# Putting the routing stretch of a two-layer trunk kernel into written order

## The chip, the cores and the metric

One core of one Trainium2 chip runs the kernel. The metric is the device time of one execution in microseconds (us); lower is better. A core has five engines with queues of their own: PE (TensorE, matrix multiplication), DVE (VectorE), ACT (ScalarE), POOL (GpSimd) and SP (SyncE, which here only issues transfers). Each works through its own queue in order and waits on semaphores for the others.

## The reference, cut to what matters

Two layers (`DEPTH = 2`) over 512 tokens of width 1024. Each adds a token mixer and then a PEER block, which alone is touched here:

```python
q = (xt @ wq).reshape(t, 8, 2, 128)
scores = einsum('thcd,hcnd->thcn', q, sub_keys)       # two times 128 keys for each of 8 heads
sv, si = top_k(scores, 16)
cand = sv[:, :, 0, :, None] + sv[:, :, 1, None, :]    # 16 x 16 sums
best_s, best_p = top_k(cand, 16)
idx  = take(si0 * 128 + si1, best_p)                  # 16 of 16384 experts for each head
gate = softmax(best_s)
act  = einsum('td,thkd->thk', x, u_tab[idx])
y    = einsum('thk,thkd->td', gelu(act) * gate, v_tab[idx])
```

Inputs and outputs are fp32; 128 (token, expert) pairs for each token.

## The kernel before

The tokens are four tiles of 128 (`t` = 0 to 3). For tiles 0 to 2 (384 tokens) the kernel doesn't gather: it multiplies them with the whole table of experts, 128 experts at a time, and a map of gates (zero where a token didn't choose an expert) selects. For tile 3 it gathers the rows of the chosen experts.

- A **U block** `e` (0 to 127): SP loads 512 KB of `peer_ut` (`uload`, L672, three buffers `u_raw`); ACT copies it to a rounded part `u_hi` and DVE subtracts to get `u_lo` (`uprep`, L677, two buffers each); PE runs 24 matmuls of 128x384 (`uact`, L702: in turn `xh`*`u_hi`, `xl`*`u_hi`, `xh`*`u_lo`); ACT applies gelu and, for `e` < 60, its queue issues the store of the result to DRAM (`ge`, L712).
- **Selection** (`stage2(t)`, L771) for the tiles in the order 3, 0, 1, 2, nearly all on DVE: candidate sums (L777 to 785), for each of 8 heads five instructions for the best 16 (L792 to 796), softmax and the arithmetic that takes a position apart (L799 to 822, with one exp on ACT), comparison and summing trees over 4096 columns (L825 to 840), normalisation (L841 to 844). For tiles 0 to 2 PE transposes the result (L852, L853) and DVE casts it to bf16 (L855 to 860: `idxT`, `gateT`).
- **Gate maps** (`onehots(t)`, L863): 24 batches of 16 tokens. DVE builds two comparison maps `oeq` and three maps `oag` of 128x2048 bf16 for a batch (L875, L879). PE multiplies them four tokens at a time, 12 matmuls of 128x128 (L885; here called a quad, four to a batch); ACT moves each quad to a staging tile `st` (L888). After two batches, a **chunk**, ACT's queue stores 2 MB to `gd` (L890).
- **Gathers** for tile 3 (`gather_u`, L731): POOL gathers one row per token (512 KB) into one of four buffers, DVE multiplies it with the token and sums it into `act` (L736). Buffers 0 and 1 of the four are the scores' own tile `sbuf`, free once selection has read it.
- **V phase** (from L969): the remaining U blocks and 128 V blocks (`vmm`, L957), written by hand under `tc.manual_schedule()`.

Up to L910 the order on each engine comes from the tile framework's scheduler, which takes instructions that it thinks ready by priority and an estimate of durations. The program only sets a pace: each `yield` of `stage2` and `onehots` gives a credit (`W_S`, `W_O / 2`), and `paced` (L893) writes a U block into the program each time the credit reaches one. By L910 that makes 69 blocks (33 beside selection, 36 beside the maps); four more (69 to 72) stand at L970, before the first V block. The V phase below is executed in its written order.

Of the kernel before, what the change touches and what calls it, by code (L numbers as in the profile page):

```python
# [7 lines left out]
F32 = mybir.dt.float32  # L8
F32R = mybir.dt.float32r
BF16 = mybir.dt.bfloat16  # L10
# [7 lines left out]
P = 128  # L18
# [29 lines left out]
W_S = 1.25  # L48
W_O = 0.75
G_R = 1  # L50
G_B = 1
# [16 lines left out]
def trunk_kernel(ctx: ExitStack, tc: tile.TileContext, x, norm1_g, w_in, sb_qn_g, sb_kn_g, ml_conv_w,  # L68
# [598 lines left out]
    def layer(l):  # L667
        with ExitStack() as pctx:
# [8 lines left out]
            def uprep(e):  # L677
                if e < NK:
                    uh = pools["up"].tile([P, ND, P], F32R, name="u_hi")
                    ul = pools["up"].tile([P, ND, P], F32R, name="u_lo")  # L680
                    src = uraw.pop(e)
                    nc.scalar.activation(uh, src, AF.Copy)  # L682
                    nc.vector.tensor_sub(ul, src, uh.bitcast(F32))  # L683
                    uT[e] = (uh, ul)
# [79 lines left out]
            with ExitStack() as bctx:  # L764
# [4 lines left out]
                pace = {"e": 0, "credit": 0.0}  # L769

                def stage2(t):  # L771
                    sv, si = svs[t], sis[t]
# [13 lines left out]
                    yield W_S  # L786
                    bs = tk.tile(HK, F32, name="bs", bufs=2)
                    bp = tk.tile(HK, U32, name="bp", bufs=2)
                    for h in range(PH):
                        c1 = cand[:, h]  # L790
                        c2 = tk.tile([P, 64], F32, name="c2", bufs=2)
                        nc.vector.max(bs[:, h, :8], c1)  # L792
                        nc.vector.max_index(bp[:, h, :8], bs[:, h, :8], c1)
                        nc.vector.match_replace(c2, bs[:, h, :8], c1, LOW)  # L794
                        nc.vector.max(bs[:, h, 8:], c2)
                        nc.vector.max_index(bp[:, h, 8:], bs[:, h, 8:], c2)
                        if h % 4 == 3:
                            yield W_S
# [24 lines left out]
                    yield W_S  # L823
# [6 lines left out]
                    yield W_S  # L830
# [3 lines left out]
                    yield W_S  # L834
# [10 lines left out]
                    if t == NT - 1:  # L845
                        nc.vector.tensor_scalar(ii[:, 0], ii[:, 0], float(NK), float(l * NE), op0=ALU.mult,
                                                op1=ALU.add)
                        nc.vector.tensor_add(idx, ii[:, 0], ii[:, 1])
                        return
                    pt = ps.tile([P, S], F32, name="tr", bufs=1)  # L850
                    for c in range(2):
                        nc.tensor.transpose(pt[:, c * P:(c + 1) * P], ii[:, c], ident)  # L852
                    nc.tensor.transpose(pt[:, 2 * P:3 * P], gt.rearrange("p h k -> p (h k)"), ident)  # L853
                    ts_ = slice(t * P, (t + 1) * P)
                    nc.vector.tensor_copy(idxT[:, :, ts_], pt[:, :2 * P].rearrange("p (c t) -> p c t", c=2))  # L855
                    gr = tk.tile([P, P], F32, name="gr", bufs=2)
                    nc.vector.tensor_copy(gateT[:, 0, ts_], pt[:, 2 * P:3 * P])
                    nc.vector.tensor_sub(gr, pt[:, 2 * P:3 * P], gateT[:, 0, ts_])
                    nc.vector.tensor_copy(gateT[:, 1, ts_], gr)
                    nc.vector.tensor_sub(gateT[:, 2, ts_], gr, gateT[:, 1, ts_])  # L860
                    yield W_S

                def onehots(t):  # L863
                    QS = [P, OT // 2, NK, 2]
                    for c in range(P // TC):
                        st = stg.tile([P, NK, TC], F32, name="st")
                        for b in range(TC // OT):
                            t0 = t * P + c * TC + b * OT

                            def pairs(row):  # L870
                                return row[:, t0:t0 + OT].rearrange("p (q b) -> p q b", b=2)[:, :, None, :].to_broadcast(QS)

                            eq = oh.tile([P, 2] + QS[1:], BF16, name="oeq")
                            for i in range(2):
                                nc.vector.tensor_tensor(eq[:, i], iota_t[:, None].to_broadcast(QS), pairs(idxT[:, i]),  # L875
                                                        op=ALU.is_equal)
                            ag = [oh.tile(QS, BF16, name="oag", bufs=4) for _ in range(3)]
                            for i in range(3):
                                nc.vector.tensor_mul(ag[i], eq[:, 0], pairs(gateT[:, i]))  # L879
                            for b4 in range(OT // 4):  # L880
                                pg = ps.tile([P, 4, NK], F32, name="oh", bufs=3)
                                for k in range(4):
                                    q, r = divmod(b4 * 4 + k, 2)
                                    for i in range(3):
                                        nc.tensor.matmul(pg[:, k, :], eq[:, 1, q, :, r], ag[i][:, q, :, r],  # L885
                                                         start=(i == 0), stop=(i == 2))
                                o = b * OT + b4 * 4
                                nc.scalar.activation(st[:, :, o:o + 4].rearrange("p i t -> p t i"), pg, AF.Copy)  # L888
                                yield W_O / 2
                        nc.scalar.dma_start(gd[t * (P // TC) + c, :, :NK * TC],  # L890
                                            st.rearrange("p i t -> p (i t)"))

                def paced(steps):  # L893
                    for n, w in enumerate(steps):
                        pace["credit"] += w
                        while pace["credit"] >= 1 and pace["e"] < UB:
                            uphase(pace["e"], ps)
                            pace["e"] += 1
                            pace["credit"] -= 1
                        yield n  # L900

                for _ in paced(w for t in (NT - 1, *range(NT - 1)) for w in stage2(t)):
                    pass
                tkctx.close()
                with ExitStack() as octx:
                    oh = octx.enter_context(tc.tile_pool(name="oh", bufs=2))
                    stg = octx.enter_context(tc.tile_pool(name="stg", bufs=2))
                    for n in paced(w for t in range(NT - 1) for w in onehots(t)):
                        gather(G_B * (n % 2))
                u_tail = pace["e"]  # L910

            with ExitStack() as cctx:
# [55 lines left out]
                with tc.manual_schedule():  # L968
                    uload(u_tail + 2)  # L969
# [66 lines left out]
```

## Time and profile before

| | |
|---|---|
| median of 3 runs | 3234.32 us (3233.31 to 3236.99) |
| the profiled execution's own time | 3247.25 us |
| its span | 3245.5 us |
| PE busy | 3142.2 us (97%) |
| DVE busy | 2480.4 us (76%) |
| ACT busy | 1381.0 us (43%) |
| POOL busy | 679.9 us (21%) |
| granted PE clock, mean | 0.98 of full speed |

The shares are means over very different stages. The change touches one stage in each layer, some 420 us long; it is the rows of that stage, which stand further down, that have to be read. In every row of a timeline the first number is the start from the span's beginning, the second the duration, both in us; in square brackets stands how long the engine was idle before and what released it. Successive instructions of one engine overlap by a little: the distance between two starts is what an instruction costs its queue.

### The profile page before, as it was taken

To read this page: it belongs to the slowest core of one execution; us is meant where nothing else is said; L and a number is where in the kernel's file an instruction comes from. 1 tells how busy PE (TensorE), PEld (TensorE's weight loads), DVE (VectorE), ACT (ScalarE), POOL (GpSimd) and SP (SyncE) were. 2 spreads that over 40 slices of the span, in tenths; PEclk is the share of its full clock that TensorE was granted. 3 is DMA by queue.
4 is the path that set the end of the run, shared out by engine and by line. 5 is a ranking of instruction groups with operands and counts; after the bars stand their busy time and mean duration, and the time that the engine had idled before them with its cause. 6 is when DMAs were issued, how large, how long until landed. Compare 5 with 4: busy or idle time off the path is not lost.

```text
span 3245.5 us, 46361 instructions
## 1 busy us (share of the span) xinstructions
PE 3142.2 (97%) x17496; PEld 2784.1 (86%) x17496; DVE 2480.4 (76%) x4655; ACT 1381.0 (43%) x2002; POOL 679.9 (21%) x563
## 2 busy tenths in 40 slices
PE   8999999899999999999989999998999999999999
PEld 8787889799888888888888778897998888888888
DVE  4756899797677777777747578998976777777777
ACT  4553334366433333333355533333664333333333
POOL 1000002430133332333200000023301333333332
PEclk9989999899999999999999999999999999999999
DMA  4202326886799998999732113268867999989997
GB/s 140 66 30 65 106 82 208 288 327 226 275 322 317 313 327 306 318 323 317 255 112 66 35 59 108 90 219 285 324 236 273 322 315 312 325 307 325 322 313 262
DMA packets 329345, 748.49 MB, mean 231 GB/s; under 512 B 26404, under 2 KB 191328, under 8 KB 326048
## 3 DMA queue, kind: packets, MB, share of 16 engines
q1 hardware_dynamic: 233632, 401.76, 37.1%
q0 software_dynamic: 74752, 269.84, 24.0%
q10 hardware_dynamic: 20736, 73.93, 5.8%
q8 instruction: 137, 2.24, 0.3%
q14 instruction: 88, 0.72, 0.1%
HBM read 669.41 MB, written 76.02 MB: 230 GB/s over the span
## 4 chain that ended last, share of the span: by engine, by line
PE 81%; DVE 10%; issue 3%; ACT 3%; POOL 2%; DMA 1%; SPq 0%; POOLq 0%; DVEq 0%; ACTq 0%
PE y L965 32%; PE act L707 23%; PE mm L185 13%; PE oh L885 3%; PE mm L531 3%; DVE u_lo L683 2%; DVE oag L879 1%; PE zz L365 1%; POOL rows L733 1%; PE zz L651 1%; PE zz L465 1%; PE y L476 1%; PE y L398 1%; PE zz L390 1%; POOL sbuf L733 1%
## 5 line engine op out<-in xcount | busy, mean ns | idle before, releaser
L707 PE MATMUL act<-xh,u_lo 128*128 128x384 f32 x2048 | 702.0, 343 | 27.0 <-DVE u_lo L683 26.6
L707 PE MATMUL act<-xh,u_hi 128*128 128x384 f32 x2048 | 703.8, 344 | 6.8 <-ACT st L888 3.7
L707 PE MATMUL act<-xl,u_hi 128*128 128x384 f32 x2048 | 698.4, 341 | 0.0
L965 PE MATMUL y<-v_hi,wh 128*128 128x512 f32 x1536 | 599.4, 390 | 3.9 <-ACT wh L952 3.9
L965 PE MATMUL y<-v_lo,wh 128*128 128x512 f32 x1536 | 599.5, 390 | 0.7 <-DVE v_lo L953 0.7
L965 PE MATMUL y<-v_hi,wl 128*128 128x512 f32 x1536 | 598.8, 390 | 0.0
L951 ACT ACTIVATE v_hi<-v_raw 128x1024 fp32r<-128x1024 f32 x256 | 272.1, 1063 | 650.9 <-issue 586.2
L683 DVE TENSOR_TENSOR u_lo<-u_raw,u_hi 128x1024 fp32r<-128x1024 f32 x256 | 310.8, 1221 | 222.5 <-ACT u_hi L682 219.7
L953 DVE TENSOR_TENSOR v_lo<-v_raw,v_hi 128x1024 fp32r<-128x1024 f32 x256 | 313.0, 1223 | 164.2 <-ACT v_hi L951 160.7
L707 PEld LDWEIGHTS act<-xh,u_lo 128*128 128x128 f32 x2048 | 389.7, 190 | 35.6 <-DVE u_lo L683 34.5
L707 PEld LDWEIGHTS act<-xh,u_hi 128*128 128x128 f32 x2048 | 389.6, 190 | 12.9 <-ACT st L888 4.0
L707 PEld LDWEIGHTS act<-xl,u_hi 128*128 128x128 f32 x2048 | 389.7, 190 | 5.0 <-issue 0.7
L682 ACT ACTIVATE u_hi<-u_raw 128x1024 fp32r<-128x1024 f32 x256 | 270.6, 1058 | 268.5 <-PE act L707 262.9
L965 PEld LDWEIGHTS y<-v_hi,wl 128*128 128x128 f32 x1536 | 289.1, 188 | 61.1 <-DVE wl L954 0.5
L965 PEld LDWEIGHTS y<-v_hi,wh 128*128 128x128 f32 x1536 | 288.9, 188 | 60.8 <-ACT wh L952 4.5
L965 PEld LDWEIGHTS y<-v_lo,wh 128*128 128x128 f32 x1536 | 289.0, 188 | 57.2 <-DVE v_lo L953 1.3
L733 POOL DMA_INDIRECT sbuf<-in_peer_u_dram,idx x128 | 176.6, 1380 | 672.7 <-DVE sbuf L736 552.2
L733 POOL DMA_INDIRECT rows<-in_peer_u_dram,idx x128 | 176.2, 1376 | 639.3 <-DVE c L794 353.6
L710 ACT ACTIVATE gelu<-act 128x384 f32<-128x384 f32 x256 | 124.2, 485 | 284.2 <-PE act L707 283.8
L888 ACT ACTIVATE st<-oh 128x512 f32<-128x512 f32 x192 | 203.9, 1145 | 86.9 <-PE oh L885 86.9
L744 POOL DMA_INDIRECT sbuf<-in_peer_v_dram,idx x128 | 157.6, 1232 | 317.9 <-DVE x_sb L747 293.0
L744 POOL DMA_INDIRECT rows<-in_peer_v_dram,idx x128 | 151.4, 1182 | 317.9 <-DVE x_sb L747 295.9
(295 smaller groups left out, 5178.5 us busy)
## 6 DMA issues: line engine op xcount, KB each, us to landing
u_raw<-in_peer_ut_dram SPq DMA_DIRECT2D x256, 512.0 KB
v_raw<-in_peer_v_dram SPq DMA_DIRECT2D x256, 512.0 KB
gd<-st ACTq DMA_DIRECT2D x24, 2048.0 KB
gt<-gd SPq DMA_DIRECT2D x64, 768.0 KB
ge<-gelu ACTq DMA_DIRECT2D x120, 192.0 KB
gelu_r<-ge SPq DMA_DIRECT2D x120, 192.0 KB
w_raw<-in_w_in_dram SPq DMA_DIRECT2D x28, 768.0 KB
w_raw<-in_peer_wq_dram SPq DMA_DIRECT2D x20, 768.0 KB
```

The costliest lines, as they stand in the source:

```text
L185: nc.tensor.matmul(ps, a_sel(a[ah], d), b_sel(b[bh], d), start=(d == 0 and i == 0), stop=(d == n - 1 and i == 2))
L531: nc.tensor.matmul(pt, yT[ah][:, b, t * P:(t + 1) * P], wo[bh][:, b, hs], start=(b == 0 and m == 0), stop=(b == n - 1 and m == 2))
L682: nc.scalar.activation(uh, src, AF.Copy)
L683: nc.vector.tensor_sub(ul, src, uh.bitcast(F32))
L707: nc.tensor.matmul(pa[:, :TD], a[:, d, :], b[:, d, :TD], start=(d == 0 and i == 0), stop=(d == ND - 1 and i == 2))
L710: nc.scalar.activation(gelu[e], pa[:, :TD], AF.Gelu_apprx_tanh)
L733: nc.gpsimd.indirect_dma_start(out=r, out_offset=None, in_=u_rows, in_offset=bass.IndirectOffsetOnAxis(ap=idx[:, p:p + 1], axis=0))
L744: nc.gpsimd.indirect_dma_start(out=r, out_offset=None, in_=v_rows, in_offset=bass.IndirectOffsetOnAxis(ap=idx[:, p:p + 1], axis=0))
L888: nc.scalar.activation(st[:, :, o:o + 4].rearrange("p i t -> p t i"), pg, AF.Copy)
L951: nc.scalar.activation(vh, vraw[e], AF.Copy)
L953: nc.vector.tensor_sub(vl, vraw.pop(e), vh.bitcast(F32))
L965: nc.tensor.matmul(ya[2 * t + half], a[:, tsl], b[:, hs], start=(k == 0 and i == 0), stop=(k == NK - 1 and i == 2))
```

## The change

1. **Written order.** Selection, maps, quads and U blocks of the stretch now stand under `tc.manual_schedule()`, so that each engine executes them as they stand in the program. `paced` and `onehots` become `credit(w)`, `make_maps(b, step)` and `quad(b, b4)`.
2. **Pace.** `stage2` yields nine times a tile (four times in the heads instead of twice, and once at the end), each worth 0.83; the maps' steps are worth 0.42. There are 37 credits in selection and 4 + 96 in the maps: 30 U blocks beside selection, 40 beside the maps (up to quad 89 of 0 to 95), 70 in all; three stand before the V phase.
3. **Transposes and casts late.** A tile's transposes are written at the head of the next tile's `stage2`, its casts behind that tile's candidate sums.
4. **Maps one batch ahead.** While PE takes the four quads of batch `b`, DVE builds batch `b + 1` in four steps (both `oeq`, then one `oag` in each). `oag` has six buffers instead of four, the quads' PSUM tile five instead of three.
5. **Gathers** are written behind every second quad, 48 in all as before, and stay there on DVE's queue.
6. `uload` runs one block further ahead; `uprep` takes an engine, which is DVE as before.

```diff
-W_S = 1.25
-W_O = 0.75
+W_S = 0.83
+W_O = 0.42
+AGB = 6
...
-            def uphase(e, ps):
-                if e:
-                    uload(e + 2)
-                uprep(e + 1)
+            def uphase(e, ps, eng):
+                uload(e + 3)
+                uprep(e + 1, eng)
                 uact(e, ps)
...
                 def stage2(t):
+                    todo_late = [f() for f in late]
+                    late.clear()
...
-                    yield W_S
+                    yield
+                    for f in todo_late:
+                        f()
...
-                        if h % 4 == 3:
-                            yield W_S
+                        if h % 2 == 1:
+                            yield
...
+                    def turn():
+                        pt = ps.tile([P, S], F32, name="tr", bufs=1)
...
+                        def casts():
...
+                        return casts
+                    late.append(turn)
...
+                def make_maps(b, step):
+                    if b >= n_bat:
+                        return
+                    if step == 0:
+                        eq = oh.tile([P, 2] + QS[1:], BF16, name="oeq")
+                        maps[b] = (eq, [])
+                        for i in range(2):
+                            nc.vector.tensor_tensor(eq[:, i], iota_t[:, None].to_broadcast(QS), pairs(idxT[:, i], b),
+                                                    op=ALU.is_equal)
+                    else:
+                        eq, ag = maps[b]
+                        ag.append(oh.tile(QS, BF16, name="oag", bufs=AGB))
+                        nc.vector.tensor_mul(ag[-1], eq[:, 0], pairs(gateT[:, step - 1], b))
...
+                def credit(w):
+                    pace["credit"] += w
+                    while pace["credit"] >= 1 and pace["e"] < UB:
+                        uphase(pace["e"], ps, nc.vector)
+                        pace["e"] += 1
+                        pace["credit"] -= 1
...
+                with tc.manual_schedule():
+                    for t in (NT - 1, *range(NT - 1)):
+                        for _ in stage2(t):
+                            credit(W_S)
+                    casts = [f() for f in late]
+                    credit(W_S)
+                    for f in casts:
+                        f()
+                    tkctx.close()
...
+                        for step in range(4):
+                            make_maps(0, step)
+                            credit(W_O)
+                        for b in range(n_bat):
+                            for b4 in range(QB):
+                                quad(b, b4)
+                                make_maps(b + 1, b4)
+                                credit(W_O)
+                                gather(G_B * (b4 % 2))
```

## Rows read from the trace of the kernel before

**Rows 1.** Busy time of each engine in four stretches of layer 0's routing (start:end, length, then PE, PE's weight loads, DVE, ACT, POOL with their instruction counts, granted PE clock, share of the DMA engines, GB/s).

```profile
447.00:602.00 155.00, 143.70 (x779) 139.99 (x779) 140.04 (x495) 58.42 (x77) 41.79 (x27) 0.96 0.66 225
602.00:640.00 38.00, 30.83 (x218) 29.11 (x218) 33.31 (x41) 15.05 (x19) 10.09 (x7) 0.87 0.63 213
640.00:735.00 95.00, 94.46 (x834) 88.12 (x834) 94.45 (x102) 62.43 (x70) 31.86 (x18) 1.00 0.89 327
735.00:847.00 112.00, 109.43 (x990) 102.29 (x988) 85.22 (x75) 74.43 (x84) 0.00 (x0) 1.00 0.59 216
```

**Rows 2.** Timeline of PE, the first matmul of a U block and the first of the V phase, in layer 0 and in layer 1.

```profile
447.15 0.44 PE L707 MATMUL act<-xh,u_hi 128*128 128x384 f32 x1 [0.69 <-ACT sc L654]
...
867.54 0.49 PE L965 MATMUL y<-v_hi,wh 128*128 128x512 f32 x1 [1.94 <-ACT wh L952]
...
2064.62 0.44 PE L707 MATMUL act<-xh,u_hi 128*128 128x384 f32 x1 [0.69 <-ACT sc L654]
...
2484.99 0.50 PE L965 MATMUL y<-v_hi,wh 128*128 128x512 f32 x1 [1.94 <-ACT wh L952]
```

**Rows 3.** What PE waited for from 447 to 868 us (total, times, longest, us).

```profile
PE act L707 <- DVE u_lo L683: 13.3, 7, 5.1
PE oh L885 <- DVE oag L879: 5.0, 6, 3.4
```

**Rows 4.** Groups of DVE's instructions from 447 to 615 us (count; busy us, mean ns; idle before, and what ended it).

```profile
L736 DVE SCALAR_TENSOR_TENSOR rows<-rows,xg 128x1024 f32<-128x1024 f32 x14 | 17.0, 1223 | 13.8 <-DMA rows<-in_peer_u_dram,idx 13.8
L827 DVE TENSOR_TENSOR eq<-abb,iota_ak 128x4096 bf16<-128x4096 bf16 x4 | 9.1, 2285 | 0.0
```

**Rows 5.** Timeline of ACT: results of two successive U blocks, and the stores of two successive chunks.

```profile
853.06 0.49 ACT L710 ACTIVATE gelu<-act 128x384 f32<-128x384 f32 x1 [6.10 <-PE act L707]
853.45 1.05 ACT L682 ACTIVATE u_hi<-u_raw 128x1024 fp32r<-128x1024 f32 x1
857.26 0.49 ACT L710 ACTIVATE gelu<-act 128x384 f32<-128x384 f32 x1 [2.76 <-PE act L707]
...
828.34 0.33 ACTq L890 DMA_DIRECT2D gd<-st  x1
...
847.00 0.33 ACTq L890 DMA_DIRECT2D gd<-st  x1
```

**Rows 6.** Timeline of PE behind two waits, and the piece of the chain of waits that holds the four U blocks before the V phase.

```profile
605.23 0.61 PE L707 MATMUL act<-xh,u_lo 128*128 128x384 f32 x1 [3.16 <-DVE u_lo L683]
605.63 0.53 PE L707 MATMUL act<-xh,u_hi 128*128 128x384 f32 x1
605.95 0.53 PE L707 MATMUL act<-xl,u_hi 128*128 128x384 f32 x1
...
572.13 0.45 PE L707 MATMUL act<-xh,u_lo 128*128 128x384 f32 x1 [1.12 <-DVE u_lo L683]
572.41 0.34 PE L707 MATMUL act<-xh,u_hi 128*128 128x384 f32 x1
572.59 0.34 PE L707 MATMUL act<-xl,u_hi 128*128 128x384 f32 x1
...
847.02 18.59 PE act L707 x96
```

**Rows 7.** Timeline of DVE in selection, where the scheduler alternates two heads: from one head's first instruction to the next head's.

```profile
483.29 0.22 DVE L792 MAX8 bs<-cand 128x8 f32<-128x64 f32 x1
483.43 0.21 DVE L795 MAX8 bs<-c 128x8 f32<-128x64 f32 x1
...
484.14 0.22 DVE L792 MAX8 bs<-cand 128x8 f32<-128x64 f32 x1
```

**Rows 8.** Timeline of DVE: two small instructions, the second on the result of the first.

```profile
212.96 0.17 DVE L148 SCALAR_TENSOR_TENSOR rq_b<-rq_b,rq_m 128x8 f32<-128x8 f32 x1
213.16 0.17 DVE L149 SCALAR_TENSOR_TENSOR rc<-rq_b,rc 128x8 f32<-128x8 f32 x1
```

**Rows 9.** Timeline of DVE: the subtraction that belongs to the copy at 853.45, and the end of the scoring before selection.

```profile
854.53 1.23 DVE L683 TENSOR_TENSOR u_lo<-u_raw,u_hi 128x1024 fp32r<-128x1024 f32 x1 [7.41 <-ACT u_hi L682]
...
452.10 0.28 DVE L663 FIND_INDEX8 sbuf<-sbuf,s 128x8 uint32<-128x128 f32 x1
```

**Rows 10.** Timeline of ACT: a gelu, the issue of its store, and the table load and exp of selection.

```profile
505.00 0.47 ACT L710 ACTIVATE gelu<-act 128x384 f32<-128x384 f32 x1
505.50 0.33 ACTq L712 DMA_DIRECT2D ge<-gelu  x1
505.86 1.28 ACT L802 ACT_TABLE_LOAD   x1 [0.39 <-ACT gelu L710]
510.62 0.31 ACT L802 ACTIVATE gt<-gt 128x128 f32<-128x128 f32 x1 [3.48 <-DVE gt L801]
```

**Rows 11.** Timeline of ACT: the gelu of the 32nd U block.

```profile
602.22 0.47 ACT L710 ACTIVATE gelu<-act 128x384 f32<-128x384 f32 x1
```

**Rows 12.** Timeline of DVE beside the maps: a gather's product and, behind it and another, two maps.

```profile
682.09 1.21 DVE L736 SCALAR_TENSOR_TENSOR rows<-rows,xg 128x1024 f32<-128x1024 f32 x1
...
684.38 2.36 DVE L879 TENSOR_TENSOR oag<-oeq,gateT 128x2048 bf16<-128x2048 bf16 x2
```

**Rows 13.** Timeline of ACT: two successive quads moved out.

```profile
642.51 1.13 ACT L888 ACTIVATE st<-oh 128x512 f32<-128x512 f32 x1 [0.21 <-PE oh L885]
643.39 1.22 ACT L888 ACTIVATE st<-oh 128x512 f32<-128x512 f32 x1
```

More of the change, by code (lines that the diff above doesn't have):

```diff
@@ L769, in layer @@
                 pace = {"e": 0, "credit": 0.0}
+                late = []
                 def stage2(t):
+                    todo_late = [f() for f in late]
+                    late.clear()
                     sv, si = svs[t], sis[t]
@@ L833, in stage2 @@
                                          .to_broadcast([P, 2 * PH * K, K // 2, 2]))
-                    yield W_S
+                    yield
                     w = K
@@ L848, in stage2 @@
                         nc.vector.tensor_add(idx, ii[:, 0], ii[:, 1])
+                        yield
                         return
[L850 to L904, printed above, removed]
@@ new lines, in stage2, with pairs @@
+                    late.append(turn)
+                QS = [P, OT // 2, NK, 2]
+                QB = OT // 4
+                n_bat = TD // OT
+                maps, sts = {}, {}
+                def pairs(row, b):
+                    row = row[:, b * OT:(b + 1) * OT].rearrange("p (q b) -> p q b", b=2)
+                    return row[:, :, None, :].to_broadcast(QS)
+                def make_maps(b, step):
[11 more added lines that the diff above has]
+                        nc.vector.tensor_mul(ag[-1], eq[:, 0], pairs(gateT[:, step - 1], b))
@@ new lines, in quad @@
+                def quad(b, b4):
+                    c, o = divmod(b * OT, TC)
+                    o += b4 * 4
+                    if o == 0:
+                        sts[c] = stg.tile([P, NK, TC], F32, name="st")
+                    st = sts[c]
+                    eq, ag = maps[b]
+                    pg = ps.tile([P, 4, NK], F32, name="oh", bufs=5)
+                    for k in range(4):
+                        q, r = divmod(b4 * 4 + k, 2)
+                        for i in range(3):
+                            nc.tensor.matmul(pg[:, k, :], eq[:, 1, q, :, r], ag[i][:, q, :, r],
+                                             start=(i == 0), stop=(i == 2))
+                    nc.scalar.activation(st[:, :, o:o + 4].rearrange("p i t -> p t i"), pg, AF.Copy)
+                    if o + 4 == TC:
+                        nc.scalar.dma_start(gd[c, :, :NK * TC], sts.pop(c).rearrange("p i t -> p (i t)"))
+                    if b4 == QB - 1:
+                        del maps[b]
```

28 lines of the change are left out of this document (18 added, 10 removed).

## The prediction

> **What bounds the kernel now.** I read the page's engine shares first: PE is busy 97% of the span, so only time in which PE idles or runs slowly can be won. Then the stretches of the stage that changes [rows 1]: PE idles 11 of 155 us beside selection and 7 of 38 us between selection and maps, at granted clocks of 0.96 and 0.87; beside the maps it is all but full. From the first U block to the first V matmul the stage takes 420.4 us in layer 0 and 420.4 us in layer 1 [rows 2], so one sum serves for both. What ends PE's idle time is DVE [rows 3]: 13.3 us for `u_lo`, 5.0 us for `oag`. Behind that stand the gathers: DVE sat 13.8 us in front of their products, waiting for rows [rows 4], with `u_lo` queued behind.
>
> How much of it can go? A U block costs 4.2 us (two gelus, 853.06 and 857.26), and a chunk without gathers 18.66 us for three blocks and eight quads, so eight quads cost 18.66 - 12.6 = 6.06 us [rows 5]. 73 blocks (306.6), 96 quads (72.7) and three groups of transposes (2.0) make 381 us. Some 39 us in each layer are waits and half clock. Of the clock the rows say: behind a wait of 3.16 us matmuls start 0.32 us apart, behind one of 1.12 us 0.18, the two levels of 1.2 and 2.4 GHz; and four blocks behind a wait of 1.83 us (the last eviction) took 18.6 us instead of 17.0 [rows 6].
>
> **The change part by part.** No work is added: the same blocks, quads, maps and gathers. What changes is who stands before whom, so I follow the written order, above all DVE's queue: pieces, `u_lo` of the next block, pieces.
>
> *What a piece costs in written order.* Instructions on DVE that don't need each other start 0.08 us before the one ahead ends (483.29 + 0.22, next 483.43) [rows 7]; one that needs the result right ahead starts 0.03 us behind its end (212.96 + 0.17, next 213.16) [rows 8]: 0.11 us more. The scheduler alternates two heads, so a head costs 0.85 us [rows 7]. Written out head by head, three of its five instructions need the one ahead: 0.85 + 3 x 0.11 = 1.2 us, a pair 2.4. By the same count candidates cost 0.85 us, the softmax and position step (some twenty instructions of about 0.2 us, seven dependent) 3.5, the comparison 2.5 and its product 2.2 (2.29 each [rows 4]), the trees and normalisation 3.5, casts 1.4.
>
> [...]
>
> *What a `u_lo` waits for.* In written order ACT runs gelu of the block that just ended, the issue of its store, then `u_hi`, then DVE `u_lo`. Gelu to `u_hi` is 0.39 us and to `u_lo` 1.47 without the store [rows 5, 9]; with it the next instruction comes 0.86 us behind the gelu [rows 10]. With 0.2 us until the gelu starts, `u_lo` starts at the earliest 2.15 us after the former block's end. It must start by 3.26 (4.2 + 0.35 until the third matmul, - 1.23 - 0.06), or PE waits. So DVE may be late by 1.1 us, and waits where it is early. Behind a waiting `u_lo` on DVE are the next pieces; behind PE's wait everything.
>
> *Selection, 30 blocks.* The credit of 0.83 leaves steps 1, 6, 12, 18, 24, 30 and 36 without a block. The stalls of PE:
> - Start: `u_lo(1)` now stands behind tile 3's candidates and two heads. Scoring ends on DVE at about 451.7 (452.10 [rows 9], less the candidate sums mixed into it); + 0.85 + 2.4 = 455.0. PE ends block 0 at 451.4 and resumes at about 455.9: 4.5 us, and half clock behind it 2.0.
> - Twice the position step and the comparison fall together: 3.5 + 2.5 + 1.14 = 7.2 us against 4.2 + 1.1: 1.9 us, clock 1.0.
> - Twice two pairs of heads: 0.6 and 0.75 us.
> - Twice the exp alone: the table load (1.28) and the exp (0.31) [rows 10] stand ahead of `u_hi`: 2.15 + 1.6 against 3.26: 0.5 us. (The other two fall where DVE is later still.)
> - Twice (tiles 0 and 2) the transposes stand before the next block and wait for the trees, written behind `u_lo`: 2.15 + 1.14 + 3.5 = 6.8 us against 4.2: with what overlaps 2.3 us, clock 1.8.
>
> Sum: 6.5 + 5.8 + 1.35 + 1.0 + 8.2 = 22.9 us. With 30 blocks (126) and transposes (2.0) selection ends at 447.15 + 150.9 = 598.0; two more blocks run while DVE casts and builds the first maps, without a stall: 32 blocks at 606.4. Before they were done at 602.2 [rows 11]: 4.2 us worse.
>
> *Maps, 41 blocks and 96 quads.* A chunk of PE work is now 3.36 x 4.2 + 6.06 = 20.2 us. DVE has ten maps, 3.36 `u_lo` and four products at 1.14 to 1.15 us apart [rows 12]: 19.8 us, 98% of it. So PE stays the bound only if neither waits for the other. They do. ACT evicts the quads (0.9 us apart [rows 13]) ahead of the next `u_hi`, so `u_lo` starts 2.5 us after its block begins, and what is behind it on DVE comes late. If a batch's last block stands at quad 1 (5 of 24), two maps and a product come behind: the next batch's first quad is ready at 2.5 + 4.7 = 7.2 us, PE at 4.2 + 1.5 = 5.7: 1.46 us. If it stands at quad 2 there is one map: 4.9 against 4.95, nothing, except in three batches where DVE arrives 1.4 us late from a long interval: 1.43 us. At quad 3 nothing is behind it. Sum 7.3 + 4.3 + 0.5 for small change = 12.1 us. What such a stall costs in clock no row shows: between none (1.12 us wait) and 1.6 us (1.83 us wait); I take 0.1 each, as after 1.12, to which it is nearer: 0.7.
>
> *Nothing:* SP's queue holds only `u_raw` loads, freed by the same `u_lo`. POOL holds only gathers, four ahead of DVE, that is two batches. The transfers of a 20.2 us chunk (3.36 loads, 4 gathers, 2 MB, 3.36 results, about 6.6 MB) ask for 326 GB/s; 640 to 735 us moved 327 with PE full [rows 1]. If that cover went, DVE would wait with `u_lo` behind. The V phase starts with 51 gathers done instead of 52.
>
> *The end* stays: the last eviction 1.83, half clock 1.6, `wh` 1.94 [rows 2, 6]: 5.4 us. If the last chunk's store and reload became the bound with three blocks behind it instead of four, up to 4 us more; no wait for it shows, so I take none.
>
> *Sum:* 606.4 + 41 x 4.2 + 72.7 + 12.1 + 0.7 + 5.4 = 869.5 us for the first V matmul; before 867.5. Between the 32nd block and the V phase before loses 867.5 - 602.2 - 244.9 = 20.4 us, now 12.8 + 5.4 = 18.2: 2 us won there, 4.2 lost in selection. + 2 us a layer, + 4 us in all: 3251 us for the profiled execution's 3247.25. That execution was 12.9 us above the median of 3234.32, so 3238 us.
>
> **The rivals.**
> - **B, faster: dependent instructions cost nothing extra.** Then a head is 0.85 us and trees 3.0: start 5.8, the double step 1.2 twice without clock, exp 0.5 twice, transposes 3.4 twice, pairs none: 16.0 instead of 22.9, - 7 us a layer: 3224 us. If the store's issue doesn't hold ACT either, `u_lo` starts 0.48 us earlier and some 5.5 us more go: 3213. For it: the dependent rows are few and of another stage. Against it: they agree.
> - **C, slower: the clock falls at every stall of 1.4 us,** as it did behind 1.83. Place: the first quad of eight batches and the double steps. Price: 8 x 1.5 + 1.3 = 13.3 us a layer: 3265 us. It decides if the granted clock falls behind waits of 1.4 us too. Against it: 1.12 cost nothing.
> - **D: the written order hardly differs from the scheduler's:** 3234. Against it: the gathers leave selection in any case.
>
> **How the numbers follow.** Forecast 0.40 (its own range 3229 to 3247, from the unseen end and half of the clock), B 0.36, C 0.18, D 0.06. The likeliest is 3238, between gain and loss. The range reaches from B with its addition (3213, and a little under) to C: 3211 to 3265, about 0.08 left out at each end. A measurement of this kernel tells 0.2% (6.5 us) from no change. Faster takes B and a little of the forecast's lower end, 0.36; slower takes C and the forecast's upper third, 0.32; the same 0.32.
>
> **What would show it.** Right: PE waits for `u_lo` of 4 to 5 us at the start, of 2 us at two groups of transposes; `oag` waits of 1.4 us at eight batches; no DVE wait for gathered rows; heads 1.2 us apart; the first V matmul near 869 us. B is right if heads lie 0.85 us apart, C if quads behind such waits run at half clock. Wrong altogether: a DVE wait for gathers beside the maps, or `u_raw` loads that come late.

## The result: 3270.8 us, 1.1% slower, and the profile after

The changed kernel takes 3270.78 us (median of 4 runs, 3268.25 to 3275.03); before takes 3234.14 us (4 runs beside it). The ratio is 1.0109, 95% interval 1.0097 to 1.0122. The forecast of 3238 us was wrong, and so was its upper end of 3265. The profiled execution took 3270.60 us, which is also the kernel's median (span 3268.9 us).

Where the time went is read from the stage first. First matmul of a U block and of the V phase, in both layers, as in [rows 2]:

```profile
439.66 0.44 PE L708 MATMUL act<-xh,u_hi 128*128 128x384 f32 x1 [0.69 <-ACT sc L655]
...
875.15 0.79 PE L1002 MATMUL y<-v_hi,wh 128*128 128x512 f32 x1 [10.80 <-ACT wh L989]
...
2074.54 0.44 PE L708 MATMUL act<-xh,u_hi 128*128 128x384 f32 x1 [0.69 <-ACT sc L655]
...
2508.64 0.80 PE L1002 MATMUL y<-v_hi,wh 128*128 128x512 f32 x1 [9.77 <-ACT wh L989]
```

The stretch of layer 0 takes 435.5 us; it was 420.4. Layer 1's first U matmul comes at 2074.54, so its stretch takes 434.1, 13.7 us more. The wait in front of the V phase has grown from 1.94 to 10.80 us, and the matmul behind it takes 0.79 us, where it took 0.49. The first matmuls of the V phase run at half clock in both kernels: in layer 0 seven of them before and twelve now last over 0.55 us, where 0.39 to 0.40 is full clock; in layer 1 eight in both.

What PE waited for in the stretch, to be held against [rows 3] (total, times, longest, us):

```profile
PE oh L911 <- DVE oag L898: 14.3, 13, 2.1
PE act L708 <- DVE u_lo L684: 11.1, 7, 4.8
PE y L1002 <- ACT wh L989: 10.8, 1, 10.8
PE tr L861 <- DVE ii L845: 4.0, 2, 2.1
```

The waits for `u_lo` have fallen only from 13.3 to 11.1; those for `oag` have risen from 5.0 to 14.3; the one for `wh` is the 10.80 us seen above; those of the transposes are new. Busy time by stage (selection, maps, from the last quad's store to the V phase; columns as in [rows 1]):

```profile
439.66:600.80 161.14, 145.45 (x780) 141.93 (x781) 139.14 (x463) 60.44 (x75) 3.99 (x4) 0.95 0.47 153
600.80:851.35 250.55, 235.06 (x2064) 227.18 (x2062) 232.00 (x251) 153.30 (x174) 79.21 (x47) 0.98 0.84 294
851.35:875.15 23.80, 12.98 (x72) 12.66 (x72) 5.97 (x10) 4.84 (x7) 3.75 (x4) 0.84 0.98 338
```

In the last 24 us PE works 13, and the DMA engines are busy for 98%: this is the only one of the three stages where they are full.

**A ledger for all kernels.** To compare kernels I take the work of PE out of each part of the stretch (4.2 us a U block, 72.7 for the quads, 2.0 for the transposes; the prediction's numbers). What is left is loss (a loss a little under zero says that the price of the work is that much too high). *Selection* ends with the gelu of the 32nd block, *maps* with the issue of the last chunk's store, *end* with the first V matmul. Layer 0, in us; U blocks ahead of the last store are 70 (69 in before, e3 and e11), 73 ahead of the V phase in all.

| kernel | median | selection | maps | end | sum |
|---|---|---|---|---|---|
| before (first profile, e0's) | 3234 to 3239 | 18.7, 17.4 | 16.7, 14.9 | 3.7, 3.8 | 39.1, 36.1 |
| forecast for the change | 3238 | 22.9 | 12.8 | 5.4 | 41.1 |
| the change | 3270.8 | 24.8 | 18.2 | 11.2 | 54.2 |
| e1 `u_lo` 1 early | 3265.5 | 22.0 | 18.5 | 11.3 | 51.8 |
| e2 no gathers late | 3253.4 | 25.2 | 17.0 | 3.8 | 46.0 |
| e3 four blocks last | 3270.7 | 24.9 | 22.0 | 8.7 | 55.5 |
| e4 transposes late | 3263.3 | 19.3 | 18.2 | 12.8 | 50.3 |
| e5 maps written only | 3240.9 | 6.9 | 19.6 | 10.5 | 37.1 |
| e6 selection written only | 3311.5 | 70.7 | -0.4 | 5.4 | 75.7 |
| e7 respaced | 3233.8 | 2.9 | 24.4 | 7.1 | 34.5 |
| e8 early `u_hi` | 3227.6 | 21.9 | -0.5 | 10.8 | 32.2 |
| e9 gathers early | 3267.6 | 23.2 | 25.8 | 3.6 | 52.6 |
| e10 = e7 + e8 | 3195.2 | 0.6 | 4.2 | 7.1 | 11.9 |
| e11 before + early `u_hi` | 3233.3 | 20.9 | 11.9 | 2.8 | 35.7 |

So the change added 6 to 7 us of loss in selection, 2 to 3 in the maps and 7.5 at the end of layer 0. In layer 1 it loses 23.1, 19.7 and 9.9 us, where before's two profiles lose 18.2 to 19.5, 14.3 to 15.9 and 3.6 to 3.7: some 4 to 5, 4 to 5 and 6 us more.

### The profile page after: what moved, and what is told of

Same layout as the page of the kernel before. It is cut to its first block, busy times and chain, and to the rows that moved or that the text cites. A ratio compares the mean times of both kernels' runs of the same rounds, so it can differ in the third digit from the quotient of the medians.

```text
span 3268.9 us, 46327 instructions
## 1 busy us (share of the span) xinstructions
PE 3129.5 (96%) x17496; PEld 2786.5 (85%) x17496; DVE 2512.9 (77%) x4655; ACT 1386.5 (42%) x2002; POOL 693.3 (21%) x563
## 3 DMA queue, kind: packets, MB, share of 16 engines
q1 hardware_dynamic: 233632, 401.76, 37.1%
## 4 chain that ended last, share of the span: by engine, by line
PE 81%; DVE 10%; ACT 5%; issue 2%; DMA 2%; ACTq 0%; SPq 0%; POOL 0%; DVEq 0%; POOLq 0%
PE y L1002 32%; PE act L708 25%; PE mm L186 13%; PE mm L532 3%; DVE u_lo L684 2%; PE oh L911 2%; DVE oag L898 2%; ACT st L913 1%; PE zz L366 1%; ACT u_hi L683 1%; PE zz L652 1%; PE zz L466 1%; PE y L399 1%; PE y L477 1%; DMA gd<-st 1%
## 5 line engine op out<-in xcount | busy, mean ns | idle before, releaser
L683 ACT ACTIVATE u_hi<-u_raw 128x1024 fp32r<-128x1024 f32 x256 | 271.9, 1062 | 31.6 <-ACT gelu L711 14.9
L744 POOL DMA_INDIRECT rows<-in_peer_v_dram,idx x128 | 161.0, 1258 | 338.6 <-DVE x_sb L747 313.1
L913 ACT ACTIVATE st<-oh 128x512 f32<-128x512 f32 x192 | 199.8, 1142 | 52.6 <-PE oh L911 51.4
```

The source lines that it names most:

```text
L744: nc.gpsimd.indirect_dma_start(out=r, out_offset=None, in_=v_rows, in_offset=bass.IndirectOffsetOnAxis(ap=idx[:, p:p + 1], axis=0))
```

## The experiments

The theory after reading the profile: each loss is a wait with a place of its own in the written order, and goes when that place is mended. The rival: DVE is busy for some nine tenths of the stretch, so that a wait taken away comes up again at the next place.

**e0: before once more.**

> The kernel before, profiled once more, to see which stretches of its first profile were long. That profile's execution took 12.9 us more than the median of its runs; the profile of the changed kernel's did not. If the 12.9 us lie in the code that the change doesn't touch (the first U matmul of layer 0 came at 447.15 us before and at 439.66 after), this profile has the first U block near 435 to 440 us and both routing stretches at 420 us again: then the whole difference of the medians, 36.6 us, belongs to the change. If they lie in the routing stretches, these are some 6 us shorter here than 420.4.

The first U matmul came at 446.93 us again, the stretches took 417.4 and 417.6, the whole 3240.65 us. So each stretch of before's first profile was 3 us longer than in this one. Where the rest of its 12.9 us lay isn't settled. The runs of before shown beside the experiments reach from 3225 to 3247 us, more than the interval of its first three told. The start of layer 0's stretch lay between 439.2 and 444.8 us in the profile of the change and its variants, in code that the change doesn't touch; I didn't pursue that.

**e1: the second block's `u_lo` ahead of selection.**

```diff
                 with tc.manual_schedule():
+                    uprep(1)
...
-                uprep(e + 1, eng)
+                if e:
+                    uprep(e + 1, eng)
```

> The u_lo of the second U block is written ahead of selection instead of behind the candidate sums and two heads of tile 3. Theory 1 (a wait of PE that is taken away is won in full): the wait of 4.8 us in front of the second block and the half clock behind it (2.0 us) go in both layers, 13 to 14 us in all: about 3257 us. Rival (the waits move: DVE is busy for nine tenths of the stretch, so it comes late at the next place instead): the wait in front of the sixth block grows from 2.1 by as much as was won, and the time stays at 3267 to 3271 us.

3265.48 us, ratio to before 1.009 (1.007 to 1.011). The wait of 4.79 us went, but one of 3.08 us came in front of the third block: 2.8 us of loss less (1.3 in layer 1), where the theory expected 6.8. Here the rival is right in part. DVE enters selection 5 us after PE (its first candidate sum starts at 444.60 in the changed kernel, PE's first matmul at 439.66), and `u_lo` of the third block now stands behind four heads.

**e2: no gathers beside the last four batches.**

```diff
-                                gather(G_B * (b4 % 2))
+                                if b < 20:
+                                    gather(G_B * (b4 % 2))
```

> No gather is written beside the last four batches of maps (40 gathers instead of 48 in the stretch; the other 8 follow in the V phase, spread over it). Theory 1: the last chunk's store took 14.1 us from issue to the issue of its reload, against 9.2 before, because five gathers were refilled beside it; without them it takes 9 to 10 us again, the wait for wh falls from 10.8 to some 5 us and the half clock behind it from 3 to 1 us: with the products gone from DVE, 7 to 9 us a layer, about 3255 us. Rival (the wait is long because only three U blocks stand behind the last quad instead of four): the wait stays at 10 us and the time within 4 us of 3271.

3253.38 us, ratio 1.0053 (1.0033 to 1.0073): 17 us won, as expected. The wait for `wh` is 2.03 us, the end loses 3.8 instead of 11.2. The chain of waits of the changed kernel runs through the last store and the first load behind its reload:

```profile
851.35 14.07 DMA gd<-st
...
865.90 7.66 DMA v_raw<-in_peer_v_dram
```

Why the store takes so long stands in the queues. ACT's store of the last chunk, SP's reload that waits for it, and POOL's gathers, then ACT and SP in e2:

```profile
851.35 0.33 ACTq L915 DMA_DIRECT2D gd<-st  x1
...
865.47 0.38 SPq L971 DMA_DIRECT2D gt<-gd  x1
865.90 1.02 SPq L974 DMA_DIRECT2D v_raw<-in_peer_v_dram  x1
...
843.87 1.68 POOL L733 DMA_INDIRECT sbuf<-in_peer_u_dram,idx  x1 [4.01 <-DVE sbuf L736]
847.29 1.68 POOL L733 DMA_INDIRECT sbuf<-in_peer_u_dram,idx  x1 [1.74 <-DVE sbuf L736]
849.28 1.99 POOL L733 DMA_INDIRECT rows<-in_peer_u_dram,idx  x1 [0.31 <-issue]
851.57 0.94 POOL L733 DMA_INDIRECT rows<-in_peer_u_dram,idx  x1 [0.30 <-issue]
852.81 0.94 POOL L733 DMA_INDIRECT sbuf<-in_peer_u_dram,idx  x1 [0.31 <-issue]
```

```profile
855.65 0.33 ACTq L915 DMA_DIRECT2D gd<-st  x1
...
864.13 0.38 SPq L972 DMA_DIRECT2D gt<-gd  x1
```

From the store's issue to the reload's: 14.1 us with five gathers (2.5 MB) refilled from 843.87 on, 8.5 without. The gathers' transfers moved 2.32 MB from 851 to 866 us in the changed kernel, 0.48 MB from 855 to 865 us in e2. In before it was 9.2 us (the store at 847.00 [rows 5]), and POOL had waited 115.1 us with full buffers until then, because the scheduler had taken the gathers early (SP's reload, and what POOL waited for in the stretch: total, times, longest):

```profile
856.22 0.91 SPq L934 DMA_DIRECT2D gt<-gd  x1
...
POOL sbuf L733 <- DVE sbuf L736: 187.5, 16, 115.1
```

And the V blocks' loads stand behind the reload on SP's queue (865.90): they are late by as much.

**e3: four blocks behind the last quad, as before.**

```diff
-                    while pace["credit"] >= 1 and pace["e"] < UB:
+                    while pace["credit"] >= 1 and pace["e"] < UB - 1:
```

> Only 69 U blocks beside selection and maps, four behind the last quad as before. If the missing fourth block made the end long: the wait for wh falls from 10.8 to 6.6 us or less, 4 to 6 us a layer, about 3261 us. If the gathers beside the last store did: the wait falls by 4.2 us as well, since a block covers it wherever it comes from, but the last six quads, which have no block between them, wait for DVE and are later by as much as the block took: less than 2 us a layer, 3267 to 3271 us.

3270.74 us, ratio 1.0111 (1.0087 to 1.0136): nothing won. The wait for `wh` fell to 8.5 and 7.1 us in the two layers, by 2.3 and 2.7 us and not by the 4.2 that both theories had, and the last batches' waits for `oag` rose (two of 2.1 us), as the gathers' theory had it: the end loses 2.5 us less and the maps 3.8 more. The number of blocks at the end isn't the cause.

**e4: transposes behind one more block.**

```diff
-                    todo_late = [f() for f in late]
-                    late.clear()
                     sv, si = svs[t], sis[t]
...
                     yield
-                    for f in todo_late:
-                        f()
+                    todo_late = [f() for f in late]
+                    late.clear()
...
                             yield
+                            for f in todo_late:
+                                f()
+                            todo_late = []
...
-                    casts = [f() for f in late]
                     credit(W_S)
+                    casts = [f() for f in late]
```

> The transposes of a tile are written behind one more U block (for tiles 0 and 1 behind the next tile's candidate sums and their block, the casts behind two heads; for tile 2 behind the block that stood after them). Theory 1 (a wait that is taken away is won): the two waits of PE of 2.0 + 0.3 us in front of transposes and about 1.4 us of half clock behind each go, 6 us a layer: 3258 to 3261 us. Rival (DVE is full and the wait comes up at the next place): the next wait for u_lo or for the first oag map grows, 3266 to 3271 us.

3263.29 us, ratio 1.008 (1.0067 to 1.0093). Both waits went and selection lost 5.5 us less in layer 0 (19.3), of which 1.6 us came back at the end; in layer 1 it lost 3.3 us less, and nothing came back at the end. A wait taken away is won here, in the main.

**e5: only the maps in written order.** `tc.manual_schedule()` opens behind selection instead of ahead of it.

> Only maps, quads, their U blocks and the gathers stand in written order; selection's order comes from the scheduler again, with the new program (pace, late transposes). If the written order is what costs selection its 6 us (161 us until the 32nd block against 155), the scheduler mixes the second u_lo with the scoring and fills DVE between heads: the 4.8 us wait at the start becomes 1.0 as before, the 32nd block comes at 150 to 153 us (no gathers stand in selection any more), and the time is 3250 to 3256 us. If the new pace and the late transposes cost it, the 32nd block stays at 160 us and the time at 3266 to 3271 us.

3240.86 us, ratio 1.0014 (1.0003 to 1.0024). The 32nd block's gelu comes at 143.3 us, earlier than expected: selection loses 6.9 us in the scheduler's order, 24.8 in the written one. In layer 1 it is 7.1 and 23.1. That says two things. The written selection costs 16 to 18 us a layer, with the same program in both. And beside the 17.4 to 18.7 of before, the changed program in the scheduler's order wins 10 to 12 us in selection. I put that down to the gathers, which have left it; but the pace and the late transposes are other too, and no run takes them apart.

**e6: only selection in written order.** The maps' part moves out of `tc.manual_schedule()`.

> Only selection stands in written order; maps, quads, U blocks and gathers are again ordered by the scheduler (with maps one batch ahead in the program, six oag buffers and five PSUM tiles). If the written order of the maps costs, the waits for oag (15 us) and for the last store go: first V matmul at 420 to 424 us instead of 435, 3243 to 3252 us. If they come from DVE being full beside the maps and from the gathers beside the last chunk, the scheduler meets the same load: within 6 us of 3271.

3311.46 us, ratio 1.0234 (1.0221 to 1.0248): neither theory had it so slow. Free to do so, the scheduler put 34 gather products between the written pieces of selection (groups of DVE's instructions, 439 to 650 us; idle before and what ended it last):

```profile
L736 DVE SCALAR_TENSOR_TENSOR rows<-rows,xg 128x1024 f32<-128x1024 f32 x24 | 29.3, 1221 | 9.7 <-DMA rows<-in_peer_u_dram,idx 9.6
L736 DVE SCALAR_TENSOR_TENSOR sbuf<-sbuf,xg 128x1024 f32<-128x1024 f32 x10 | 12.2, 1219 | 4.8 <-DMA sbuf<-in_peer_u_dram,idx 4.8
```

41.5 us of products and 14.4 us of waits for rows, with `u_lo` behind: PE waited 44.5 us for it and the first quad came at 206 us instead of 161. The maps, ordered by the scheduler, lose nothing (-0.4), but only 15 products are left beside them. So the run doesn't isolate the maps' order; it shows what gathers in a full selection cost.

**e7: written order, respaced.** Every step of selection but the candidate sums of tiles 0 to 2 gets a block, so that no two long DVE pieces share one interval; 26 gathers instead of 48 stay in the stretch (the others follow in the V phase).

```diff
+                    uprep(1)
...
-                        for _ in stage2(t):
-                            credit(W_S)
+                        for n, _ in enumerate(stage2(t)):
+                            credit(1 if n or t == NT - 1 else 0)
...
-W_O = 0.42
+W_O = 0.37
...
-                                gather(G_B * (b4 % 2))
+                                gather(int(b < 20 and (b * QB + b4) % 3 == 2))
```

The first block issues no `uprep`, as in e1, the casts stand behind two heads, and the final `credit(W_S)` is `credit(1)`.

> The written order, respaced by what was read: u_lo of the second block ahead of selection and block 0 at the first step; a U block at every step of selection but the candidate sums of tiles 0 to 2 (34 blocks there instead of 30), so that no two long DVE steps stand between two blocks; casts behind two heads; maps at 0.37 blocks a step; one gather behind every third quad up to batch 19 (26 instead of 48; the other 22 in the V phase). Theory 1 (sum of waits): the PE work of 381 us, some 4 us of waits in selection, 4 beside the maps, 6 at the end: first V matmul at 393 to 400 us, 420 before; 3185 to 3205 us, if 22 more gathers cost the V phase nothing. Rival (DVE, not the order, is the bound in selection): a tile's selection is 33.7 us of DVE with its eight u_lo against 33.6 of PE, so PE waits for u_lo all through and the 32nd block comes at 150 us or later; 3220 to 3235 us.

3233.84 us, ratio 0.9991 (0.9983 to 1.0). Selection loses 2.9 us, less than the 6.9 in the scheduler's order (e5), so the written order as such costs nothing there and DVE's load isn't the bound: the places of blocks, `u_lo` and casts were. But the maps lost 24.4 us, more than in any run before, with fewer products on DVE. DVE's load can't explain that, and it made me look at what DVE waits for.

**e8: the copy `u_hi` ahead of the evictions.** In the changed kernel, around 640 us: ACT, then DVE.

```profile
637.76 0.49 ACT L711 ACTIVATE gelu<-act 128x384 f32<-128x384 f32 x1 [1.58 <-PE act L708]
638.28 0.33 ACTq L713 DMA_DIRECT2D ge<-gelu  x1
638.66 2.10 ACT L913 ACTIVATE st<-oh 128x512 f32<-128x512 f32 x2 [0.40 <-PE oh L911]
640.79 0.33 ACTq L915 DMA_DIRECT2D gd<-st  x1
641.22 1.06 ACT L683 ACTIVATE u_hi<-u_raw 128x1024 fp32r<-128x1024 f32 x1 [0.46 <-DVE oag L898]
...
642.31 1.23 DVE L684 TENSOR_TENSOR u_lo<-u_raw,u_hi 128x1024 fp32r<-128x1024 f32 x1 [1.25 <-ACT u_hi L683]
```

The buffer of `u_hi` is free when the block ends, at 637.7. The copy stands behind the evictions of the quads that follow and a store, and starts at 641.22; DVE waits for it 1.25 us with the next maps behind; PE's quads wait for the maps; and ACT's evictions wait for the quads. The ring closes.

```diff
                 uprep(e + 1, eng)
                 uact(e, ps)
+                uhi(e + 2)
```

`uhi` is the copy alone; `uprep` then issues only the subtraction, at its old place.

> The copy u_hi of a block is written on ACT right behind the gelu of the block before the last (its buffer's last reader), ahead of the evictions of the quads that follow; u_lo stays where it is on DVE. Beside the maps DVE waited 21.7 us for u_hi in front of u_lo, with the next maps behind it. Theory (a ring: PE's quads wait for a map, the map stands on DVE behind u_lo, u_lo waits for u_hi, and u_hi stands on ACT behind the evictions of the quads): DVE's wait for u_hi falls below 8 us, PE's waits for oag from 15 to 5 us or less, and with the half clock of 3 us the last store comes 8 to 12 us earlier: 3247 to 3256 us. Rival (DVE is full beside the maps: 19.8 us of work to PE's 20.2 a chunk, so that its idle time only moves): the waits for oag stay at 12 us or more, 3264 to 3272 us.

3227.61 us, ratio 0.9982 (0.9969 to 0.9995): 43 us won, two to three times what was expected. All the waits of PE for `oag` are gone and the maps lose nothing. What DVE waited for from 600 to 840 us, in the changed kernel and in e8 (total, times, longest):

```profile
DVE u_lo L684 <- ACT u_hi L683: 18.4, 18, 2.5
```

```profile
DVE u_lo L692 <- ACT u_hi L684: 0.3, 1, 0.3
```

DVE's work is the same in both, so the rival falls. It had the load right: from 610 to 830 us of e8, DVE is busy for 219.3 of 220 us and PE for 219.95 (204.5 and 207.8 in the changed kernel). Here a full DVE didn't make PE wait; a DVE that waited for ACT did. The last store came 21.6 us earlier in layer 0, where I had expected 8 to 12: all of the `oag` waits (14.3 us) and the half clock behind them went, and some 3 us in selection.

**e9: all 48 gathers, beside the first twenty batches.**

```diff
-                                gather(G_B * (b4 % 2))
+                                n = b * QB + b4
+                                if b < 20:
+                                    gather(n % 2 + (n % 10 == 0))
```

> As many gathers as in the changed kernel (48), but all beside the first twenty batches of maps, none beside the last four; everything else stays. If the place of the gathers makes the end long (refilled beside the last store), the wait for wh falls from 10.8 to 2 us as with 40 gathers, and the eight extra products on DVE cost at most some 0.5 us each in waits for oag: 3253 to 3260 us. If their number does (DVE's or the queue's load in the whole stretch), the end's wait stays above 8 us or the waits for oag grow by the same 8 to 9 us: 3266 to 3272 us.

3267.58 us, ratio 1.0106 (1.0091 to 1.0122), which was the rival's number. The end behaved as the place theory had it (wait for `wh` 1.94 us, loss 3.6 with as many gathers): it is their place that makes the end long. But the maps lost 25.8 us. Beside e2, which differs by eight products ahead of the last store, that is 8.8 us more, or 1.1 each (1.2 in layer 1), where I had written 0.5 at most: with the ring in place each product counts about in full (1.14 to 1.15 us [rows 12]).

**e10: respaced and early `u_hi` together.**

> The respaced order together with the early u_hi. In the respaced kernel selection lost 1.9 us and the maps 18 to 20 us in waits for oag, though DVE had less to do there, and DVE waited 42 us for u_hi. If the ring through ACT makes these waits, they fall to 6 us or less here and the last store comes at 382 to 386 us instead of 396: 3203 to 3215 us. If the maps themselves are late (DVE's rate), the waits stay at 15 us or more and the time is 3228 to 3235 us.

3195.21 us (3190.98 to 3196.62), ratio 0.9883 (0.9869 to 0.9897): faster than both kernels, and than either theory had it (the last store came at 373.5 us). Its three stages:

```profile
439.77:576.80 137.03, 136.00 (x776) 134.51 (x777) 127.97 (x445) 61.01 (x76) 3.88 (x4) 1.00 0.55 176
576.80:813.25 236.45, 229.08 (x2067) 222.27 (x2065) 216.13 (x224) 154.62 (x174) 43.95 (x26) 1.00 0.75 267
813.25:832.97 19.72, 12.79 (x73) 12.47 (x73) 6.29 (x10) 4.83 (x7) 2.81 (x3) 0.92 0.88 308
```

PE works 136 of 137 us in selection at full clock, and DVE 128 of 137 without delaying it. What is left is 4.2 us in the first maps and 7.1 at the end, where the store still takes 11.8 us until its reload. Two gathers are issued beside it; in layer 1 two as well, where the store takes 8.8 us and the end still loses 6.6. What makes this end long stays open. And 22 of the gathers have moved to the V phase, so the gain isn't the order's alone.

**e11: before, with the early `u_hi` alone.** The same two edits of `uprep` and `uphase` in the kernel before.

> The kernel before, with the early u_hi alone (the copy stands in the program right behind the gelu of the block before the last; the scheduler orders everything else as it did). If the ring through ACT belongs to the written order of the change, the scheduler had already avoided it (DVE waited 9.7 us for u_hi beside the maps, against 21.7 in the changed kernel) and little is won: 3226 to 3238 us. If the ring cost the kernel before as much (its maps lost 15 to 17 us over the work of PE, the changed kernel's 18), the early copy wins some 10 us a layer here too: 3208 to 3218 us.

3233.25 us, ratio 0.9981 (0.997 to 0.9992), the number of the first theory, but not a test of it. The scheduler didn't put the copy early: from 615 to 840 us two or three evictions stand ahead of it in 23 of 34 blocks, its median start is 4.7 us behind the last gelu (5.2 in before, 0.95 in e8), and DVE waits 12.8 us for it (5.3 in before). That the ring cost before little is seen in before's own rows: from 640 us on PE is busy for 94.46 of 95 and 109.43 of 112 us [rows 1] and waits 1.0 us for `oag`, while DVE waits 19.3 us for PE. Most of what before loses in the maps lies ahead of 640. How its order keeps the copy's delay from PE isn't shown.

## Why the prediction was wrong, by its own steps

**Right: the prices of pieces, and selection place by place.** Two heads in written order start 1.26 us apart, forecast 1.2, and rival B's 0.85 is refuted (timeline of DVE, first instruction of two successive heads; then PE at the start and at one group of transposes):

```profile
445.51 0.23 DVE L797 MAX8 bs<-cand 128x8 f32<-128x64 f32 x1
...
446.77 0.20 DVE L797 MAX8 bs<-cand 128x8 f32<-128x64 f32 x1
...
449.26 0.69 PE L708 MATMUL act<-xh,u_lo 128*128 128x384 f32 x1 [4.79 <-DVE u_lo L684]
...
585.70 0.41 PE L861 MATMUL tr<-ident,ii 128*128 128x128 f32 x2 [2.07 <-DVE ii L845]
```

The start cost 4.79 us (4.5 forecast), the double steps 2.12 and 1.96 (1.9), two groups of transposes 1.98 + 0.33 and 2.07 + 0.26 (2.3). PE's waits in selection (those over 0.2 us) add up to 15.7 us, forecast 15.25; the rest is mostly half clock. Selection lost 24.8 us against 22.9.

Of the 25 us or so that the two stretches took beyond the forecast, 2 lie in selection, 12 in the maps and 10 at the end.

**Wrong: the term for the end.** "If the last chunk's store and reload became the bound with three blocks behind it instead of four, up to 4 us more; no wait for it shows, so I take none." It became the bound: the end lost 5.8 us more than the forecast's 5.4 in layer 0 and 4.5 more in layer 1, and not for the blocks (e3) but for the gathers that the change keeps refilling beside the last store (e2, e9). The paragraph "Nothing" had the premise in hand: POOL "holds only gathers, four ahead", and a chunk's transfers were compared with a rate seen beside full PE. It was done for a chunk in the middle, where a late store has 20 us; the last one has 12.6. Before's trace showed POOL idle in just that place (0.00 busy from 735 to 847 us [rows 1]); the prediction doesn't ask what its transfers would do there.

**Half right: the maps' waits.** They came in front of eight batches, as forecast, but added up to 14.3 us instead of 12.1, and the clock behind them cost 3.1 us instead of 0.7 (two blocks took 5.99 us instead of 4.42). With what else was lost there it makes 18.2 us against 12.8, and 19.7 in layer 1. "DVE has ten maps, 3.36 `u_lo` and four products ... 19.8 us, 98% of it" is right, as e8 shows with both engines full. The delay of `u_lo` is what was mis-sized: the prediction saw the evictions ahead of `u_hi` and put the start of `u_lo` at 2.5 us behind its block's start, for every block. It lay between 2.5 and 5.0 us; in e8, where the copy comes early, between 0.9 and 2.9. That the copy's place makes the waits is shown by e8, which takes them all away with DVE's work unchanged.

**Wrong: the step from the profile to the median.** "That execution was 12.9 us above the median ..., so 3238 us." On the profile's own scale the forecast was 3251 us and the execution took 3270.6: 13.1 and 11.8 us in the two stretches and 2.3 us between the first V matmul of layer 0 and the first U matmul of layer 1, less 7.5 us at the start of layer 0. The 2.3 us I can't explain: that part takes 1194.5 to 1200.7 us in the variants, and 1194.5 in e8, whose V phase starts at half clock too. The remaining 13 us is the offset that I carried over as if it were a constant; the changed kernel's profiled execution lies at its median. Without it the forecast would have been 3251 us and C 3278, above the measured time.

**The rivals.** C had the sign, not the mechanism. Its condition was that the clock falls behind waits of 1.4 us. Waits of 1.5 us cost no clock in the maps of either layer, one of 2.05 us none in layer 0; two waits of 1.08 and 0.92 us with one matmul between them did. D is refuted by e5: the two orders differ by 16 to 18 us a layer in selection alone.

**What the change was good for.** The changed program, with the gathers out of selection, wins 10 to 12 us a layer there in the scheduler's order (e5). The changed kernel paid that back in selection itself (24.8 instead of 6.9) and lost more at the end. The loss in selection lies in places: an earlier `u_lo` gives 2.8 us back (e1), later transposes 5.5 (e4), both with a block at every long step 21.9 (e7). e7 and e10 show that written order can keep the gain.

## What to carry to other kernels

Before an order is written out by hand, follow each pair of engines around once: which instruction on A waits for B, what stands ahead of B's on its queue, and does that wait for A; a copy written "where it is used" can close a ring between queues, which cost 18.7 us in layer 0's maps here (e8). That an engine's work fits the interval doesn't say that its waits do. And of a transfer that moves, price it at the last tile, where nothing covers what it delays, not in the middle.

## What the runs showed of the hardware that was not expected

The granted clock fell in places that the length of the wait alone doesn't order. In the changed kernel a wait of 2.05 us at 652.69 was followed by matmuls at full pace, two waits of 1.08 and 0.92 us by half clock; and in layer 1 a wait of the same 2.05 us, in front of the same quad, was followed by half clock:

```profile
652.69 0.74 PE L911 MATMUL oh<-oag,oeq 128*128 128x128 bf16 x10 [2.05 <-DVE oag L898]
653.24 0.42 PE L708 MATMUL act<-xh,u_hi 128*128 128x384 f32 x1
653.50 0.34 PE L708 MATMUL act<-xl,u_hi 128*128 128x384 f32 x1
653.68 0.34 PE L708 MATMUL act<-xh,u_lo 128*128 128x384 f32 x1
...
714.82 0.22 PE L911 MATMUL oh<-oag,oeq 128*128 128x128 bf16 x1 [1.08 <-DVE oag L898]
715.96 0.74 PE L911 MATMUL oh<-oag,oeq 128*128 128x128 bf16 x10 [0.92 <-DVE oag L898]
...
717.37 0.53 PE L708 MATMUL act<-xl,u_hi 128*128 128x384 f32 x1
717.69 0.53 PE L708 MATMUL act<-xh,u_lo 128*128 128x384 f32 x1
...
2286.04 0.73 PE L911 MATMUL oh<-oag,oeq 128*128 128x128 bf16 x10 [2.05 <-DVE oag L898]
...
2287.41 0.52 PE L708 MATMUL act<-xl,u_hi 128*128 128x384 f32 x1
```

At 653 the matmuls of the block last 0.34 us, at 717 and 2287 0.52 to 0.53. What decides between the two isn't shown. And a 2 MB store with 2.5 MB of gathers refilled around it needed 14.1 us until its reload could be issued, 8.5 without (12.1 and 7.2 in layer 1). The mean rate beside the maps (294 GB/s), below the 338 of the last 24 us, gave no sign of that.
